# Scores as plain fp32 products of both heads in turn, block rows computed once and shifted by transfers, and another order in the mixer of a two-layer trunk

## The chip, the cores and the metric

The kernel runs on one core of a Trainium2 chip. The metric is the device time of one execution in microseconds (us), the median of several. Five engines work beside each other, each through its own instructions in order: TensorE (PE in the profile; its weight loads are PEld), VectorE (DVE), ScalarE (ACT), GpSimd (POOL) and SyncE (SP), which here only issues transfers (DMAs).

## The reference, cut to what matters

```python
# layer 0: h = x @ w_in + b; u, q, k, v = split(h)          x: 512 x 1024, each part 512 wide
# S5 on u: 32 groups of 16 channels, a complex state of 64 per group
lam_bar = exp(lam * dt); b_bar = (lam_bar - 1) / lam * b
states = scan(s[t] = lam_bar * s[t-1] + b_bar @ u[t])
y = gelu(real(c @ states) + d * u);  s5_out = val * sigmoid(gate) of y @ w_glu + b_glu
# stick-breaking attention, 8 heads of 64
z = q @ k.T * 64 ** -0.5                                    # strictly causal
log_keep = where(strict, log_sigmoid(-z), 0)
after = sum of log_keep over the keys between a key and its query
out = where(strict, exp(log_sigmoid(z) + after), 0) @ v
# x = LN(alpha * x + concat(s5_out, out) @ w_out + b), then a squared-ReLU MLP
# layer 1: conformer convolution (GLU, depthwise conv 31, LN, swish), then the MLP again
```

## The kernel before, in words

Channels lie on the 128 partitions and the 512 time steps along the free side. Products with weights are made in three parts: a weight chunk is fetched whole (`raw`), ACT rounds it to the fp32r format (`whi`), DVE takes the rest (`wlo`), inputs are split likewise (`xh`, `xl`), and PE adds `whi*xh`, `whi*xl`, `wlo*xh`. One result of 128 x 512 takes 8 x 3 = 24 such products. Weight chunks come in the order in which the program uses them, their fetches on SP's queue.

The mixer (layer 0 up to the MLP) is the first 254 us. Its parts are written down in the string `ORDER`. `sN` is stage N of the four S5 stages (`s5_states`, 4 tiles r of 128 channels' states each): DVE makes the block matrices `Gx` and `Cx` (time is cut in blocks of 4 steps); PE transposes `Gx` (`gp`) and forms the inner block matrix `tp`, which ACT copies to `Tx`; PE makes `vR`, `vI`; DVE turns them by cosine and sine tables, scans, turns them back and writes the shifted states `Sx` (the chain of tiles `m`, `n`). `yN` (`s5_outputs`) is then `yp = Tx*U + Cx*Sx` on PE, taken into `U` by DVE. `qN` (`qkv`) makes q, k, v of a pair of heads. `aN` (`attention`) is that pair's attention: scores `z` in groups A, B, C of key blocks for each head; `sp` = softplus of z (ACT: Abs, Exp, Ln; DVE: one addition; POOL: the causal mask), its parts `sh`, `sl`; `weigh` adds on PE the sums after each key; ACT takes Exp (`w`), POOL masks, and `values` makes the product with v (`av`). `gelu` works on all stages' `U` and turns the layout by way of DRAM (`Yd`, `yf`, parts `yh`, `yl`); `glu` is the S5 output projection (`gg`, `gv`); `acmo` are the products of the output projection. `ATT` gives the order of scores (s), weighing (w) and values (v) within one attention.

A scheduler places instructions of parts that stand near each other in the program on the engines, so that products of one part stand between those of another; the engines then run that order.

Of the kernel before, what the change touches and what calls it, by code (L numbers as in the profile page):

```python
# [16 lines left out]
P = 128  # L17
T = 512
# [29 lines left out]
ATT = "sC0 sA0 sB0 sB1 wC0 wB0 sC1 wB1 vB sA1 wA0 wC1 vC wA1 vA"  # L48
MIX_BUFS = (3, 4, 1, 4, 3)
WARM = 24  # L50
QK_BUFS = (1, 1)
TABLES_FIRST = (0, 1, 2, 3)
ORDER = "q0 s0 y0 s1 y1 a0 rows q1 s2 y2 a1 s3 y3 q2 gelu a2 q3 glu a3".split()
# [112 lines left out]
def kernel(ctx: ExitStack, tc: tile.TileContext, a: dict, out: bass.AP):  # L166
# [87 lines left out]
    def zz(name):  # L254
        return psum("z", name, MIX_BUFS[1])

# [22 lines left out]
    with tc.high_priority():  # L279
        for j in range(KT):  # L280
            tag, bufs = (("spt", MIX_BUFS[3]), ("wt", MIX_BUFS[4]), ("qh", 1))[(0, 1, 0, 1, 0, 1, 0, 2)[j]]
            xt = att.tile([P, 4, P], F32, tag=tag, name=f"xin{j}", bufs=bufs)
            nc.sync.dma_start(xt, a["x"][0][:, P * j : P * (j + 1)].rearrange("(b p) f -> p b f", p=P))
            xin.append(xt)
# [71 lines left out]
    def stt(o, x, s, y, op0, op1):  # L356
        V.scalar_tensor_tensor(o, x, s, y, op0=op0, op1=op1)  # L357
        return o
# [147 lines left out]
    def s5_states(q):  # L506
# [18 lines left out]
        for r in range(4):  # L525
            for t in range(4):
                for i in range(2):
                    PE.matmul(tp[32 * t : 32 * t + 32, r * P + 32 * t : (r + 1) * P],
                              Gx[:, i, r, 3].rearrange("p g q -> p (g q)"),
                              Cx[:, i, r, 0 : 4 - t].rearrange("p t g q -> p (t g q)"),  # L530
                              start=i == 0, stop=i == 1, tile_position=(0, 32 * t))
        tpv = tp.rearrange("p (r c) -> p r c", r=4)
        for t in range(4):
            pp = slice(32 * t, 32 * t + 32)
            S.copy(Tx[pp, :, 32 * t :], tpv[pp, :, 32 * t :])
# [92 lines left out]
    def qkv(p):  # L628
        r = []
        for s, n in enumerate("qkv"):  # L630
            ps, b = in_proj(4 + 4 * s + p, f"{n}{p}")
            if s == 2:
                t_ = att.tile([P, T], F32, tag=n, name=f"{n}{p}")
                act(t_, ps, AF.Identity, bias=b)
            else:
                b = b if s else bq8[:, p : p + 1]
                t_ = tuple(att.tile([P, T], F32R, tag=n + x, name=f"{n}{x}{p}", bufs=QK_BUFS[s]) for x in "hl")
                act(t_[0], ps, AF.Identity, bias=b)
                stt(t_[1], ps, b, t_[0].bitcast(F32), ALU.add, ALU.subtract)
            r.append(t_)  # L640
        return r
# [3 lines left out]
    def attention(p, q_, k_, v_):  # L645
# [21 lines left out]
        def scores(g):  # L667
            z = zs[g] = zz(f"z{p}{g}")
            for h, kb, o in groups[g]:
                R = slice(64 * h, 64 * h + 64)  # L670
                for i, (u, v) in enumerate(((0, 0), (0, 1), (1, 0))):
                    ins = PE.matmul(z[:, o : o + T - P * kb], k_[u][R, P * kb : P * kb + P], q_[v][R, P * kb :],
                                    start=o == 0 and i == 0, stop=i == 2, skip_group_check=True).ins
                    if o or i:
                        tc.add_manual_dep(ins, opened, NOSYNC, reason="the bank's first product")
                    opened = ins.name
            n = H if g[0] == "C" else T
            z = z[:, :n]
# [6 lines left out]
            hi = att.tile([P, n], F32R, tag=f"sh{g[0]}", name=f"sh{p}{g}", bufs=1)  # L685
            lo = att.tile([P, n], F32R, tag=f"sl{g[0]}", name=f"sl{p}{g}", bufs=1)
# [558 lines left out]
```

## Time and profile before

| | |
|---|---|
| median of 3 runs | 1217.15 us (1216.98 to 1217.62) |
| profiled execution | 1217.5 us, its span 1215.8 us |
| PE busy | 1187.4 us, 98% of the span |
| PEld, DVE, ACT, POOL busy | 83%, 65%, 46%, 5% |
| chain that ended last | PE 83%, DVE 10%, ACT 4%, DMA 2% |

The span lies within the execution; 1.7 us are around it. A matmul's duration in the trace is its time from issue to its modelled end, and the next starts before that; what one costs PE is the distance from its start to the next start. A plain fp32 matmul stands in the trace as two instructions, an fp32r one as one.

### The profile page before, as it was taken

The numbers are of one execution on the slowest core, as the hardware profiler recorded it, in microseconds if no ns is written. First come the engines' busy times: TensorE is split into PE (matmuls) and PEld (weight loads), VectorE is DVE, ScalarE is ACT, GpSimd is POOL, SyncE is SP. The second block draws the span as 40 slices with busy tenths as digits, with TensorE's granted clock in tenths as the row PEclk, the third lists the DMA queues.
The fourth block names the chain that finished last, engine by engine and source line by source line (L and its number), as shares of the span: only waits on it lengthen the run. The fifth ranks groups of instructions, "written<-read, shape, count | busy, mean of one in ns | idle before, by whom it ended". The sixth has DMA issues, their size and how long they took to land.

```text
span 1215.8 us, 16751 instructions
## 1 busy us (share of the span) xinstructions
PE 1187.4 (98%) x6546; PEld 1007.5 (83%) x6546; DVE 786.9 (65%) x1400; ACT 557.1 (46%) x990; POOL 58.2 (5%) x125
## 2 busy tenths in 40 slices
PE   9899999999999999999999999899999999999997
PEld 7677776789988888888999888889988888888885
DVE  7998774578745635646566999998843443434446
ACT  6836665734525524425323456964651332323230
POOL 1001101100000000000022110102000000000000
PEclk9999999999999999999999999999999999999999
DMA  8510042150878787887454631406142232323211
GB/s 205 155 49 22 19 130 61 31 195 1 264 250 282 251 284 264 270 283 268 165 183 159 213 104 36 139 1 208 39 152 87 87 108 83 122 70 121 70 52 69
DMA packets 128943, 168.86 MB, mean 139 GB/s; under 512 B 11298, under 2 KB 101666, under 8 KB 128864
## 3 DMA queue, kind: packets, MB, share of 16 engines
q1 hardware_dynamic: 120064, 136.30, 34.5%
q0 software_dynamic: 8640, 31.46, 7.6%
q8 instruction: 51, 0.84, 0.3%
q14 instruction: 28, 0.23, 0.1%
q10 hardware_dynamic: 160, 0.03, 0.0%
HBM read 132.12 MB, written 35.65 MB: 138 GB/s over the span
## 4 chain that ended last, share of the span: by engine, by line
PE 83%; DVE 10%; ACT 4%; DMA 2%; issue 1%; POOL 0%; SPq 0%; DVEq 0%; POOLq 0%; ACTq 0%
PE f L225 23%; PE g L1175 12%; PE acf L225 11%; PE fl L225 5%; PE tld L225 4%; PE tlb L225 4%; PE h L1159 3%; PE cv L1076 2%; PE pv L225 2%; PE pg L225 2%; PE tla L225 2%; PE pl L225 2%; DVE cz L357 1%; PE acmo L225 1%; PE av L709 1%
## 5 line engine op out<-in xcount | busy, mean ns | idle before, releaser
L102 DVE TENSOR_TENSOR wlo<-raw,whi 128x1024 fp32r<-128x1024 f32 x176 | 213.4, 1224 | 199.5 <-ACT whi L101 198.7
L101 ACT CAST whi<-raw 128x1024 fp32r<-128x1024 f32 x176 | 182.1, 1049 | 313.5 <-PE g L1175 107.4
L1175 PE MATMUL g<-whi,hh 128*128 128x512 f32 x208 | 81.8, 393 | 0.0
L1175 PE MATMUL g<-wlo,hh 128*128 128x512 f32 x208 | 81.8, 393 | 0.0
L1175 PE MATMUL g<-whi,hl 128*128 128x512 f32 x208 | 81.7, 393 | 0.0
L225 PE MATMUL f<-xah,whi 128*128 128x512 f32 x208 | 81.2, 390 | 0.0
L225 PE MATMUL f<-xdl,whi 128*128 128x512 f32 x208 | 81.1, 390 | 0.0
L225 PE MATMUL f<-xah,wlo 128*128 128x512 f32 x208 | 81.0, 390 | 0.0
L225 PE MATMUL f<-xdh,whi 128*128 128x512 f32 x208 | 81.0, 390 | 0.0
L225 PE MATMUL f<-xal,whi 128*128 128x512 f32 x208 | 81.0, 390 | 0.0
L225 PE MATMUL f<-xdh,wlo 128*128 128x512 f32 x208 | 81.0, 390 | 0.0
L225 PE MATMUL acf<-hl,whi 128*128 128x512 f32 x192 | 75.7, 394 | 0.0
L225 PE MATMUL acf<-hh,wlo 128*128 128x512 f32 x192 | 75.6, 394 | 0.0
L225 PE MATMUL acf<-hh,whi 128*128 128x512 f32 x192 | 75.5, 393 | 0.0
L215 ACT CAST hh<-fr 128x512 fp32r<-128x512 f32 x64 | 39.7, 621 | 59.6 <-DVE fr L353 59.6
L216 DVE TENSOR_TENSOR hl<-fr,hh 128x512 fp32r<-128x512 f32 x64 | 44.1, 690 | 31.9 <-ACT hh L215 31.8
L357 DVE SCALAR_TENSOR_TENSOR cy<-hp,wdw,cy 128x512 f32<-128x512 f32 (+1 forms) x99 | 63.6, 654 | 0.2
L357 DVE SCALAR_TENSOR_TENSOR cz<-hp,wdw,cz 128x512 f32<-128x512 f32 (+1 forms) x93 | 60.0, 656 | 0.0
L353 DVE TENSOR_TENSOR fr<-fr 128x512 f32<-128x512 f32 x64 | 43.7, 685 | 14.7 <-ACT fr L154 14.6
L1175 PEld LDWEIGHTS g<-wlo,hh 128*128 128x128 f32 x208 | 39.1, 188 | 8.9
L1175 PEld LDWEIGHTS g<-whi,hl 128*128 128x128 f32 x208 | 39.1, 188 | 8.9
L1175 PEld LDWEIGHTS g<-whi,hh 128*128 128x128 f32 x208 | 39.1, 188 | 8.8
(684 smaller groups left out, 3093.4 us busy)
## 6 DMA issues: line engine op xcount, KB each, us to landing
raw<-in_ffn_w_dram SPq DMA_DIRECT2D x48, 1024.0 KB, 5.8
raw<-in_ffn_w_dram SPq DMA_DIRECT2D x32, 512.0 KB, 3.5
kepth<-whi SPq DMA_DIRECT2D x30, 512.0 KB, 8.6
keptl<-wlo SPq DMA_DIRECT2D x30, 512.0 KB, 9.4
whi<-kepth POOLq DMA_DIRECT2D x30, 512.0 KB, 3.7
wlo<-keptl POOLq DMA_DIRECT2D x30, 512.0 KB, 4.5
raw<-in_conv_w_pw_dram SPq DMA_DIRECT2D x12, 1024.0 KB, 6.5
raw<-in_mix_w_in_dram SPq DMA_DIRECT2D x16, 512.0 KB, 3.9
```

Of the source, the lines that this page charges most:

```text
L101: i0 = nc.scalar.copy(hi, raw).ins
L102: i1 = nc.vector.tensor_sub(lo, raw, hi.bitcast(F32)).ins
L215: i0 = S.copy(hi, src).ins
L216: i1 = V.tensor_sub(lo, src, hi.bitcast(F32)).ins
L225: ins = PE.matmul(ps[:, c0:c1], u[:, k, ksl], v[:, c0:c1], start=start and k == 0 and i == 0, stop=stop and k == n - 1 and i == 2).ins
L353: V.tensor_tensor(o, x, y, op=op)
L357: V.scalar_tensor_tensor(o, x, s, y, op0=op0, op1=op1)
L709: ins = PE.matmul(av[R, P * kb :], vt[:, kb, R], ws_[f"{c}{h}"][0][:, o : o + T - P * kb], start=summed[h] == 1, stop=summed[h] == 4, skip ...
L1076: PE.matmul(cps[j][:, c0:c1], u, v[:, t + c0 : t + c1], start=t == 0 and i == 0, stop=t == n - 1 and i == 2)
L1159: PE.matmul(ps, u, v, start=k == 0 and i == 0, stop=k == nk - 1 and i == 2)
L1175: PE.matmul(pss[b], u, v[:, kk, :], start=k + kk == 0 and i == 0, stop=k + kk == nb - 1 and i == 2)
```

## The change

Four things. `qkv` makes plain fp32 q and k by one ACT instruction each, where before ACT made the rounded part (`qh`, `kh`) and DVE the rest (`ql`, `kl`). `scores` makes for each key block one fp32 product instead of three fp32r ones, head 0 (rows 0 to 63 of PE) and head 1 (rows 64 to 127) in turn; groups C and B of both heads stand ahead of A. In `s5_states`, `tp` is made once for the first block column: 8 matmuls on 4 column groups of PE instead of 32; ACT copies it to `tk`, and 16 DMAs on SP's queue place it in `Tx`, shifted. `ORDER` is another, and some buffer counts go with it.

```diff
-ATT = "sC0 sA0 sB0 sB1 wC0 wB0 sC1 wB1 vB sA1 wA0 wC1 vC wA1 vA"
-MIX_BUFS = (3, 4, 1, 4, 3)
+ATT = "sC sB wC0 wC1 vC wB1 wB0 sA wA0 vB wA1 vA"
+MIX_BUFS = (3, 4, 1, 3, 3)
+SP_BUFS = {"A": 1, "B": 2, "C": 2}
-ORDER = "q0 s0 y0 s1 y1 a0 rows q1 s2 y2 a1 s3 y3 q2 gelu a2 q3 glu a3".split()
+ORDER = "q0 s0 a0 y0 s1 q1 y1 a1 s2 y2 rows s3 y3 q2 q3 gelu a2 glu a3".split()
...
         tp = s5ps(f"tp{q}")
-        for r in range(4):
-            for t in range(4):
-                for i in range(2):
-                    PE.matmul(tp[32 * t : 32 * t + 32, r * P + 32 * t : (r + 1) * P],
-                              Gx[:, i, r, 3].rearrange("p g q -> p (g q)"),
-                              Cx[:, i, r, 0 : 4 - t].rearrange("p t g q -> p (t g q)"),
-                              start=i == 0, stop=i == 1, tile_position=(0, 32 * t))
-        tpv = tp.rearrange("p (r c) -> p r c", r=4)
+        for i in range(2):
+            for r in range(4):
+                PE.matmul(tp[32 * r : 32 * r + 32, :P], Gx[:, i, r, 3].rearrange("p g q -> p (g q)"),
+                          Cx[:, i, r, 0:4].rearrange("p t g q -> p (t g q)"),
+                          start=i == 0, stop=i == 1, tile_position=(0, 32 * r))
+        tk = s5.tile([P, P], F32, tag=("cii", "cix")[q % 2], name=f"tk{q}")
+        S.copy(tk, tp[:, :P])
         for t in range(4):
-            pp = slice(32 * t, 32 * t + 32)
-            S.copy(Tx[pp, :, 32 * t :], tpv[pp, :, 32 * t :])
+            for r in range(4):
+                nc.sync.dma_start(Tx[32 * t : 32 * t + 32, r, 32 * t :], tk[32 * r : 32 * r + 32, : P - 32 * t])
...
-            if s == 2:
-                t_ = att.tile([P, T], F32, tag=n, name=f"{n}{p}")
-                act(t_, ps, AF.Identity, bias=b)
-            else:
-                b = b if s else bq8[:, p : p + 1]
-                t_ = tuple(att.tile([P, T], F32R, tag=n + x, name=f"{n}{x}{p}", bufs=QK_BUFS[s]) for x in "hl")
-                act(t_[0], ps, AF.Identity, bias=b)
-                stt(t_[1], ps, b, t_[0].bitcast(F32), ALU.add, ALU.subtract)
+            t_ = att.tile([P, T], F32, tag=n, name=f"{n}{p}", bufs=2 if s == 2 else QK_BUFS[s])
+            act(t_, ps, AF.Identity, bias=b if s else bq8[:, p : p + 1])
...
-        def scores(g):
-            z = zs[g] = zz(f"z{p}{g}")
-            for h, kb, o in groups[g]:
-                R = slice(64 * h, 64 * h + 64)
-                for i, (u, v) in enumerate(((0, 0), (0, 1), (1, 0))):
-                    ins = PE.matmul(z[:, o : o + T - P * kb], k_[u][R, P * kb : P * kb + P], q_[v][R, P * kb :],
+        def scores(c):
+            for h in range(2):
+                zs[f"{c}{h}"] = zz(f"z{p}{c}{h}")
+            before = None
+            for pair in zip(groups[c + "0"], groups[c + "1"]):
+                for h, kb, o in pair:
+                    R = slice(64 * h, 64 * h + 64)
+                    ins = PE.matmul(zs[f"{c}{h}"][:, o : o + T - P * kb], k_[R, P * kb : P * kb + P], q_[R, P * kb :],
+                                    start=o == 0, stop=True, skip_group_check=True).ins
+                    if before:
+                        tc.add_manual_dep(ins, before, NOSYNC, reason="both heads in turn")
+                    before = ins.name
+            for h in range(2):
+                softened(f"{c}{h}")
...
-            hi = att.tile([P, n], F32R, tag=f"sh{g[0]}", name=f"sh{p}{g}", bufs=1)
-            lo = att.tile([P, n], F32R, tag=f"sl{g[0]}", name=f"sl{p}{g}", bufs=1)
+            hi = att.tile([P, n], F32R, tag=f"sh{g[0]}", name=f"sh{p}{g}", bufs=SP_BUFS[g[0]])
+            lo = att.tile([P, n], F32R, tag=f"sl{g[0]}", name=f"sl{p}{g}", bufs=SP_BUFS[g[0]])
```

`softened` is the rest of the old `scores`: softplus, mask and split, unchanged.

DVE, stage 0, where it makes `Cx` for the first `tp`. Before:

```order
L353 TENSOR_TENSOR Gx<-cm 64x16x16 x2
L353 TENSOR_TENSOR cm<-PW,Cd 128x320 x2
L353 TENSOR_TENSOR Cx<-cm 64x20x16
L102 TENSOR_TENSOR wlo_751<-raw_748,whi_750 128x1024
L357 SCALAR_TENSOR_TENSOR kl_745<-k_719,PB,kh_744 128x512
L353 TENSOR_TENSOR Cx<-cm 64x20x16
L353 TENSOR_TENSOR cm<-PW,Cd 128x320 x2
L357 SCALAR_TENSOR_TENSOR Cx<-cm 64x20x16 x2
L353 TENSOR_TENSOR cm<-EE,Braw 128x256 x2
L102 TENSOR_TENSOR wlo_1213<-raw_1210,whi_1212 128x1024
```

Now:

```order
L354 TENSOR_TENSOR Gx<-cm 64x16x16 x2
L354 TENSOR_TENSOR cm<-PW,Cd 128x320 x2
L354 TENSOR_TENSOR Cx<-cm 64x20x16 x2
L103 TENSOR_TENSOR wlo_747<-raw_744,whi_746 128x1024
L354 TENSOR_TENSOR cm<-PW,Cd 128x320 x2
L358 SCALAR_TENSOR_TENSOR Cx<-cm 64x20x16 x2
L354 TENSOR_TENSOR cm<-EE,Braw 128x256 x2
L103 TENSOR_TENSOR wlo_1136<-raw_1133,whi_1135 128x1024
```

The piece of k (`kl`, and just ahead of these rows that of q, `ql`) is gone, and the two first halves of `Cx` stand together, ahead of the weight rest `wlo`.

SP, the queue behind the last weight chunk (`raw`) of the second pair of heads. Before, fetches alone:

```order
L71 DMA raw_1280<-in_mix_w_in_dram 128x8x128
L71 DMA raw_1721<-in_mix_w_in_dram 128x8x128
L71 DMA raw_1756<-in_mix_w_in_dram 128x8x128
L621 DMA rows<-in_s_b_glu_dram 8x128
L621 DMA rows<-in_mix_b_out_dram 8x128
```

Now:

```order
L72 DMA raw_1199<-in_mix_w_in_dram 128x8x128
L537 DMA Tx<-tk_820 32x128 x4
L537 DMA Tx<-tk_820 32x96 x4
L537 DMA Tx<-tk_820 32x64 x4
L537 DMA Tx<-tk_820 32x32 x4
L72 DMA raw_1641<-in_mix_w_in_dram 128x8x128
L537 DMA Tx<-tk_1083 32x128 x4
L537 DMA Tx<-tk_1083 32x96
L72 DMA raw_1674<-in_mix_w_in_dram 128x8x128
L537 DMA Tx<-tk_1083 32x96 x3
```

All 16 shifts of stage 0 and those of stage 1 stand between weight fetches, which wait behind them in the queue.

PE, from the end of the last stage's `yp` to the first weighing of the third pair of heads (`z2C<-sh2B`). Before, the last rows ahead of it; between them and the last `yp` stand 50 more rows, 14 of them scores and all others products of q and k of the fourth pair:

```order
L225 MATMUL k_2103<-x0l_256,whi_1793 128x512
L225 MATMUL k_2103<-x0h_255,wlo_1794 128x512
L225 MATMUL k_2103<-x0h_268,whi_1793 128x512
L225 MATMUL k_2103<-x0l_269,whi_1793 128x512
L225 MATMUL k_2103<-x0h_268,wlo_1794 128x512
L225 MATMUL v_2138<-x0h_172,whi_2064 128x512
L696 MATMUL z2C_1901<-sh2B_1943,negs 128x128
L696 MATMUL z2B_1930<-sh2B_1943,negs 128x128
```

Now, all rows behind `yp`:

```order
L226 MATMUL v_1812<-x0h_268,wlo_1743 128x512
L644 MATMUL vt_1908<-ident,v_1738 128x128 x4
L671 MATMUL z2C_1916<-q_1672,k_1705 128x256
L671 MATMUL z2C_1917<-q_1672,k_1705 128x256
L671 MATMUL z2B_1941<-q_1672,k_1705 128x384
L671 MATMUL z2B_1942<-q_1672,k_1705 128x384
L671 MATMUL z2B_1941<-q_1672,k_1705 128x128
L671 MATMUL z2B_1942<-q_1672,k_1705 128x128
L226 MATMUL gg_2073<-yh_1856,whi_1808 128x512
L226 MATMUL gg_2073<-yl_1857,whi_1808 128x512
L226 MATMUL gg_2073<-yh_1856,wlo_1809 128x512
L699 MATMUL z2C_1916<-sh2B_1953,negs 128x128
```

The 42 products of the fourth pair's q, k, v that stood ahead of the weighing are made earlier, beside stages 2 and 3; in their place stand one product of v, three of the S5 output projection (`gg`, which need `yh` and `yl`) and the scores.

## Rows read from the trace of the kernel before

**Rows 1.** The page: busy time of each engine with its share of the span, and the chain of work that ended last.

```profile
PE 1187.4 (98%) x6546; PEld 1007.5 (83%) x6546; DVE 786.9 (65%) x1400; ACT 557.1 (46%) x990; POOL 58.2 (5%) x125
PE 83%; DVE 10%; ACT 4%; DMA 2%; issue 1%; POOL 0%; SPq 0%; DVEq 0%; POOLq 0%; ACTq 0%
```

**Rows 2.** Busy time of the engines in stretches of the mixer: stretch and length, then us busy and (x instructions) of each engine, PE's granted clock as a share of full speed, DMA share, GB/s.

```profile
60.00:80.00 20.00, 19.31 (x165) 16.41 (x168) 19.62 (x37) 3.90 (x7) 0.70 (x1) 1.00 0.19 53
80.00:100.00 20.00, 18.76 (x118) 15.01 (x111) 19.16 (x35) 14.48 (x28) 2.69 (x7) 1.00 0.21 59
...
0.00:254.00 254.00, 241.24 (x1428) 187.51 (x1428) 189.71 (x410) 158.23 (x285) 26.28 (x65) 0.99 0.33 89
```

**Rows 3.** PE in order of time in stage 1 (start, us, instructions, and in brackets the idle time before with what ended it), and the group of all `tp` in the mixer (busy us, mean ns, idle).

```profile
77.94 0.83 PE L542 MATMUL vI<-U,gt 128*128 128x128 f32 x6
78.71 1.72 PE L528 MATMUL tp<-Cx,Gx 128*32 128x128 f32 x62
80.35 0.49 PE L542 MATMUL vI<-U,gt 128*128 128x128 f32 x2
...
L528 PE MATMUL tp<-Cx,Gx 128*32 128x128 f32 (+3 forms) x256 | 9.3, 259 | 2.7 <-DVE Cx L357 1.5 <-DVE Cx L353 1.3
```

**Rows 4.** PE in order of time in the last `yp`: the distance from start to start gives what a 128 x 128 fp32 instruction costs.

```profile
160.64 0.61 PE L572 MATMUL yp<-Sx,Cx 128*128 128x128 f32 x4
161.09 0.39 PE L570 MATMUL yp<-U,Tx 128*128 128x128 f32 x2
```

**Rows 5.** PE and then DVE in order of time in stage 0, and the windows view of the stretch at the lower clock.

```profile
55.09 0.38 PE L528 MATMUL tp<-Cx,Gx 128*32 128x128 f32 x2 [1.27 <-DVE Cx L353]
56.94 2.95 PE L528 MATMUL tp<-Cx,Gx 128*32 128x128 f32 x62 [1.48 <-DVE Cx L357]
...
48.81 0.75 DVE L357 SCALAR_TENSOR_TENSOR ql<-q,bq,qh 128x512 fp32r<-128x512 f32 x1
53.70 0.73 DVE L357 SCALAR_TENSOR_TENSOR kl<-k,PB,kh 128x512 fp32r<-128x512 f32 x1
55.90 0.98 DVE L357 SCALAR_TENSOR_TENSOR Cx<-cm 64x320 f32<-64x320 f32 x2
...
56.09:59.51 3.42, 2.57 (x60) 2.45 (x62) 2.68 (x5) 0.06 (x1) 0.00 (x0) 0.50 0.29 87
```

**Rows 6.** PE's busy time with score products alone, all 96 of them, then PE in order of time where the two heads of group B meet (the fourth pair), and the pair of `av` products on column halves.

```profile
sum 254.00, PE 19.14; mean PE 4.79
...
218.23 0.33 PE L672 MATMUL z3B<-qh,kl 64*128 64x384 f32 x1
218.23 0.44 PE L672 MATMUL z3B<-qh,kh 64*128 64x384 f32 x2
...
110.08 1.53 PE L709 MATMUL av<-w0A,vt 128*64 128x512 f32 x4
111.54 0.66 PE L520 MATMUL gp<-ident,Gx 128*128 128x128 f32 x4
```

**Rows 7.** DVE in order of time: the first and the last of the chain from `vR` to `Sx` in stage 0; SP's queue (issue times); and from the list of transfers KB of each and median us from issue to landing.

```profile
61.24 0.68 DVE L353 TENSOR_TENSOR m<-vR,tc 128x512 f32<-128x512 f32 x1
71.21 0.69 DVE L353 TENSOR_TENSOR Sx<-m,n 128x508 f32<-128x508 f32 x1
...
49.42 1.74 SPq L607 DMA_DIRECT2D U<-Ud  x4
...
U<-Ud SPq DMA_DIRECT2D x16, 64.0 KB, 4.4
rows<-in_ffn_b_dram SPq DMA_DIRECT2D x2, 8.0 KB, 1.8
```

**Rows 8.** From the end of the last `yp` to the first weighing of the third pair: PE, DVE, ACT and POOL in order of time, then the windows view of that stretch for the products with weights (x42) and for the scores (x14).

```profile
162.52 0.38 PE L672 MATMUL z2C<-qh,kl 64*128 64x256 f32 x1
174.73 0.27 PE L696 MATMUL z2C<-sh2B,negs 128*128 128x128 f32 x1
...
170.20 1.23 DVE L102 TENSOR_TENSOR wlo<-raw,whi 128x1024 fp32r<-128x1024 f32 x1 [1.97 <-ACT whi L101]
172.69 0.68 DVE L357 SCALAR_TENSOR_TENSOR sp2B<-z2B,sp2B 128x512 f32<-128x512 f32 x1
...
167.52 1.28 ACT L156 ACT_TABLE_LOAD   x1
174.00 0.62 ACT L215 CAST sh2B<-sp2B 128x512 fp32r<-128x512 f32 x1
...
173.44 0.53 POOL L664 TENSOR_SCALAR_AFFINE_SELECT sp2B<-sp2B 128x256 f32<-128x256 f32 x1 [0.31 <-DVE sp2B L357]
...
162.52:174.73 12.21, 9.93 (x42) 1.00 0.46 115
162.52:174.73 12.21, 2.49 (x14) 1.00 0.46 115
```

**Rows 9.** PE's waits in the first 255 us: engine, line, what it waited for, us in total, times, longest.

```profile
PE yp L572 <- DVE Sx L353: 1.9, 3, 0.7
PE z2C L672 <- ACT w2C L160: 1.2, 1, 1.2
```

**Rows 10.** The one other stretch at the lower clock, and the one ahead of it.

```profile
779.00:783.10 4.10, 0.29 (x1) 0.19 (x1) 4.10 (x12) 3.10 (x7) 1.00 (x2) 1.00 1.08 372
783.10:786.50 3.40, 3.29 (x14) 3.03 (x14) 3.21 (x10) 2.62 (x9) 0.00 (x0) 0.50 0.04 14
```

More of the change, by code (lines that the diff above doesn't have):

```diff
@@ L280 @@
         for j in range(KT):
-            tag, bufs = (("spt", MIX_BUFS[3]), ("wt", MIX_BUFS[4]), ("qh", 1))[(0, 1, 0, 1, 0, 1, 0, 2)[j]]
+            tag, bufs = (("spt", MIX_BUFS[3]), ("wt", MIX_BUFS[4]), ("q", 1), ("k", 1))[(0, 1, 0, 1, 0, 1, 3, 2)[j]]
             xt = att.tile([P, 4, P], F32, tag=tag, name=f"xin{j}", bufs=bufs)
@@ L665, in mask, with softened @@
                                    base=0, channel_multiplier=-1).ins.name
-        def scores(g):
-            z = zs[g] = zz(f"z{p}{g}")
-            for h, kb, o in groups[g]:
-                R = slice(64 * h, 64 * h + 64)
-                for i, (u, v) in enumerate(((0, 0), (0, 1), (1, 0))):
-                    ins = PE.matmul(z[:, o : o + T - P * kb], k_[u][R, P * kb : P * kb + P], q_[v][R, P * kb :],
[L673 to L676, printed above, removed]
+        def scores(c):
[12 more added lines that the diff above has]
+                softened(f"{c}{h}")
+        def softened(g):
             n = H if g[0] == "C" else T
-            z = z[:, :n]
+            z = zs[g][:, :n]
             sp = att.tile([P, T], F32, tag="spt", name=f"sp{p}{g}", bufs=MIX_BUFS[3])[:, :n]
```

## The prediction

> **What bounds the kernel now.** I read the page first: PE is busy for 98% of the span and carries 83% of the chain that ended last [rows 1]. So a change is worth what it takes from PE's work, or from PE's waits. The windows view then says where PE waits at all: of the first 254 us, which hold the whole mixer and everything that changes, PE works 241.2 [rows 2]; the rest of the kernel keeps its instructions. In the same windows DVE works 19.6 and 19.2 of 20 us between 60 and 100 us. There DVE is nearly as full as PE, and work taken from it can start PE sooner. Last I read PE's waits by what ended them: for `Sx` 1.9 us, for `w2C` 1.2, and little for any other [rows 9]. PE is filled so well because each chain of DVE and ACT lies beside products of q, k and v that need nothing from it. The change moves just these products, so besides the work removed the question is which chain stays without cover.
>
> All sums are made against the profiled execution's own 1217.5 us; the median of the runs shown, 1217.15, lies 0.35 below it, and I take that off at the end.
>
> **Inner block matrix.** All 256 instructions of `tp` keep PE busy for 9.3 us [rows 3]. In stage 1, 62 of them take 78.71 to 80.35, 1.64 us. One 128 x 128 fp32 instruction costs about 0.11 us from start to start (4 begin at 160.64, the next at 161.09) [rows 4]. The widths of `tp` are 128, 96, 64 and 32, so 62 in a row would take 62 x 80/128 x 0.11 = 4.3 us. It goes 2.6 times faster: the four column groups run at once. The group with the widest products alone (16 of 128 columns, 1.8 us) would take what all take, so the time looks like that of the longest group. After the change each stage has 16 instructions of 128 columns, four on each column group: 0.45 us if the groups go on running together, 1.8 if they do not. By the row nearest to it I take 0.55, four stages 2.2. At full clock `tp` now costs about 7.5 (the 9.3 hold some 1.8 of stage 0, which is slow for another reason, below). **Gain 5.3**, bounds 0.3 and 5.7.
>
> The copies to `Tx` leave ACT, and 16 DMAs each stage take their place. Four small DMAs take SP 1.74 us to issue, 0.43 each, so 16 take 6.9; such transfers land 1.8 (8 KB) to 4.4 us (64 KB) after issue [rows 7]; the new ones have 16 KB at most, and I take 2. `Tx` is wanted by `yp`, which also waits for `Sx`: that chain takes DVE 61.24 to 71.9, over 10 us, in stage 0 [rows 7]. 6.9 + 2 = 8.9 is hidden behind it by about 1 us, so I cost it at nothing. If the cover is gone (a weight fetch between two shifts, which waits for its buffer and holds SP's queue), what is late next is `yp`, then `U` on DVE; that is a rival below.
>
> **Start of stage 0.** PE stands for 1.27 and 1.48 us ahead of `tp`, both times for `Cx` [rows 5]. On DVE the rests of q and k, 0.75 and 0.73 us, stand ahead of the last `Cx`; both go, so `Cx` comes 1.5 us sooner: **gain 1.5** (bounds 0.7, if ACT is late next, and 2.75, the whole wait). [...] I expect the wait that is left, some 1.3 us with 16 instructions behind it, not to bring it: **gain 1.3** (bounds 0 and 1.3). The other six rests of q and k give DVE 4.5 us more room in stretches where it is full; PE's 1.9 us for `Sx` are what this can reach, and I count 1.
>
> **Scores.** The 96 score instructions, 24 for a pair of heads, keep PE busy for 19.1 us [rows 6]; since each runs past the start of the next, by starts it is about 18, or 4.5 a pair. After the change a pair has 8 matmuls, 16 instructions, 1280 columns a head. At the pitch of [rows 4] 128 columns cost 0.22 as an fp32 matmul: 10 x 0.22 = 2.2 us a head. If the heads run one behind the other that is 4.4, almost what it is now; if they overlap fully, 2.2. Two places speak for overlap: where the heads meet in group B, instructions of both start at the same 218.23; and the two `av` products, on halves of PE's columns and plain fp32, take 110.08 to 111.54, 1.46 us, where four instructions of 512 columns would take 4 x 0.44 = 1.76 [rows 6]. That fits an order in which the second half of head 0's product and the first of head 1's run together: three units for a lone pair, two for each more in a row. Groups C and B stand together so (about 1.6 us), A's two products stand apart in three of four pairs (1.7). That is 3.3, and some 0.2 for places where another product comes between: four pairs 14, **gain 4.0** (bounds 0.3 and 9).
>
> Scores take half of PE's rows and `tp` a quarter of its columns, so PE changes between these and whole-array products. In [rows 3] six instructions of `vI` take 77.94 to 78.71, 0.77 instead of 0.66: about 0.1 us for such a change. [...] With some 20 more changes at 0.1 the sum would be 2 us worse; by the row alone, where as many changes go as come, nothing.
>
> **Order.** The costly part. From the end of the last `yp` to the first weighing of the third pair of heads, 162.52 to 174.73, 12.2 us pass now: `U`, the last block of gelu, ACT's table load for Exp at 167.52, softplus, `sh2B` at 174.00 [rows 8]. PE is busy throughout, with 42 products of q, k, v (9.9 us) and 14 of scores (2.5) [rows 8]. After the change one product of v, the transposes of v, six score matmuls and three `gg` stand there, and these last wait for `yl`, which comes after softplus too. The chain itself becomes about 1.5 longer, since a weight rest (1.23 us [rows 8]) stands between the first and the other `U` on DVE and ACT has both heads' group C ahead of B. So 13.7 us against some 5.2 of PE work (0.2 + 0.5 + 3 + 0.7, and 0.8 for a bank that frees late): **loss 8.5** (bounds 6 and 11). After a wait like this the clock falls as well: after 779.00 to 783.10, in which PE worked 0.29 us, it ran 3.40 us at 0.50 [rows 10]. That loses up to 1.7; part of it lies ahead of head 1's wait, and I count **0.9**.
>
> The products taken from there stand beside `a0` and stages 1 to 3. They are needed in any case, so they gain only what they fill: in `a0` the softplus of all groups stands behind stage 0's `Sx` on DVE. `Sx` ends near 68 (71.9 less 2.7 by the start of stage 0, less 1.2 for a weight rest that no longer stands in it); with additions 1.5, mask 0.5 and `sh2B`'s like 0.6 [rows 8] the first weighing can start near 71. PE, some 58.4 behind `vI`, has scores (2) and 35 products of 0.23 until then, to about 68.5: a wait of 2.5 to 3. Some 2 us more are new in `a1`. Against them go 1.9 and 1.2 [rows 9] and some 1.5 of smaller waits. I count nothing.
>
> **Sum.** -5.3 - 1.5 - 1.3 - 1.0 - 4.0 + 8.5 + 0.9 = -3.7 us: 1213.8 for the profiled execution, **1213.5** as a median.
>
> **Rivals.** *The order loses more than the work gives (slower).* If in `a0` and `a1` PE waits 5 us more than I count, and the wait behind the last `yp` is 11, the losses are 17.3 against gains of 13.1: +4, 1221. It decides from the point where PE's waits of these phases exceed what goes by 13. For it speaks that DVE is full between 60 and 100 us [rows 2], where `a0` now stands; against it, that DVE has 6 us less to do. *Shifts late (no change).* If fetches hold the queue so that `Tx` comes 1 to 1.5 us after `Sx` in three stages, 4 us go: 1217.5. [...] *Heads do not overlap (no change).* Then scores gain 0.3 instead of 4: 1217.2. *Heads overlap fully (more).* 2.2 a pair saves 9: 1208.5.
>
> **How the numbers follow.** The measurement can tell 0.2%, 2.4 us, from no change. Forecast 0.40 (of which 0.34 faster, 0.06 within), full overlap 0.10, shifts late 0.12, no overlap 0.08, order loses more 0.30. So faster 0.44, same 0.26, slower 0.30. The range reaches from full overlap with a smaller wait behind `yp` (1208.5 less 3, 1205.5) to the order's loss with the clock's whole loss on top (1221 and 2, 1223); the forecast's own is 1210 to 1216.5.
>
> **What would show it.** `tp` at or below 0.6 us a stage; in stage 0 one wait for `Cx` and no stretch at 0.50; scores at 3 to 3.6 us a pair, starts of both heads within 0.02 us; `yp` waiting for `Sx`, never for a DMA; one PE wait of 7 to 10 us behind the last `yp`, ended by `sh2B` or `yl`, with a slow stretch behind it. I am wrong if that wait is much shorter because the scheduler's filler or the chain differs from what I counted, or if PE waits over 5 us in `a0` or `a1`.

## The result and the profile after

The change made the kernel slightly slower: 1219.3 us in the median of 13 runs (1218.35 to 1224.55) beside 1217.13 for the kernel before on the same chip, a ratio of 1.0021 (95% interval 1.0012 to 1.0029), or 1.5 to 3.5 us. The forecast was 1213.5.

The profiled execution took 1218.93 us, its span is 1217.2. From the page and the windows view of the changed kernel (columns as in [rows 1, 2]):

```profile
PE 1183.1 (97%) x6322; PEld 998.9 (82%) x6322; DVE 779.9 (64%) x1392; ACT 552.3 (45%) x978; POOL 60.7 (5%) x125
...
0.00:254.00 254.00, 235.45 (x1198) 178.14 (x1199) 182.56 (x402) 152.99 (x273) 28.89 (x65) 0.97 0.33 90
```

In the first 254 us PE is busy 5.8 us less than in [rows 2], DVE 7.2 and ACT 5.2 less, and yet the mixer is longer. Its end is best read at the first product behind it: it starts at 255.07 us before and at 256.44 now, 1.4 later. From there to the end it is 960.7 and 960.8 us, so all of the difference lies in the mixer.

The busy time hides how much work went, since a product at a granted clock of 0.50 counts longer: in after a 128x512 fp32r product takes 0.43 us from start to start at 0.50 (72.50 to 72.93) and 0.23 at 1.00 (40.05 to 40.28). Counted from start to start, without idle time and with time at the lower clock by half, PE's work in the mixer fell from 240.2 to 231.0 us. That is 9.2 less; the forecast had 9.3. What came in its place is 5.8 us of waiting and 4.8 us lost to the clock. By stretches (this table is worked out from the starts and ends of PE's instructions in both traces, in us):

| term | forecast | measured |
|---|---|---|
| work: `tp` | -5.3 | -4.6 (7.7 to 3.1) |
| work: scores | -4.0 | -1.3 (17.9 to 16.6) |
| work: `av` -2.0, weighing -0.7, rest -0.6 | 0 | -3.3 |
| waits and clock up to the end of the last `yp` | -3.8 | +0.6 (10.0 to 10.5) |
| waits and clock from there to the first weighing of pair 2 | +8.5 | +8.1 (0 to 8.1) |
| waits and clock behind it | +0.9 | +1.9 (3.4 to 5.3) |
| sum | -3.7 | +1.4 |

**The stretch behind the last `yp`.** PE in order of time in the changed kernel, then the windows view (the long wait, what follows at the lower clock, and behind it):

```profile
168.25 0.61 PE L574 MATMUL yp<-Sx,Cx 128*128 128x128 f32 x4
168.62 0.48 PE L226 MATMUL v<-x0h,wlo 128*128 128x512 f32 x1
168.94 0.60 PE L644 MATMUL vt<-ident,v 128*128 128x128 f32 x4
169.46 0.70 PE L671 MATMUL z2C<-q,k 64*128 64x256 f32 x4
170.87 1.51 PE L671 MATMUL z2B<-q,k 64*128 64x384 f32 x8 [0.70 <-ACT vt L646]
178.85 0.80 PE L226 MATMUL gg<-yh,whi 128*128 128x512 f32 x1 [6.47 <-ACT yh L155]
...
180.67 0.37 PE L699 MATMUL z2C<-sh2B,negs 128*128 128x128 f32 x1
...
168.70:180.67 11.97, 4.79 (x22) 2.74 (x21) 8.72 (x23) 10.15 (x21) 1.32 (x3) 0.72 0.62 168
178.85:187.50 8.65, 8.61 (x29) 7.24 (x30) 4.57 (x8) 4.84 (x10) 2.43 (x4) 0.50 0.39 121
187.50:191.00 3.50, 3.50 (x13) 1.36 (x12) 0.00 (x0) 1.81 (x4) 0.49 (x2) 0.99 0.00 0
```

This is the place that the prediction spoke of: one product of v, the transposes, the scores, and then one wait of 6.47 us. The stretch takes 11.97 us now and took 12.2 before [rows 8], although PE's busy time in it fell from the whole of it to 4.79. So it is not PE that sets its length. ACT is busy for 10.15 of it, and ACT and DVE do one thing after another:

```profile
170.33 0.86 DVE L358 SCALAR_TENSOR_TENSOR U<-U,par,yp 128x128 f32<-128x128 f32 x3
174.18 0.69 DVE L358 SCALAR_TENSOR_TENSOR g<-g,U 128x512 f32<-128x512 f32 x1 [0.39 <-ACT g L161]
...
174.17 1.28 ACT L157 ACT_TABLE_LOAD   x1
178.18 0.61 ACT L155 ACTIVATE yh<-yf 128x512 fp32r<-128x512 f32 x1
179.90 0.62 ACT L216 CAST sh2B<-sp2B 128x512 fp32r<-128x512 f32 x1 [0.32 <-POOL sp2B L660]
```

`U`, the last block of gelu, the table load for Exp and softplus are the chain of before; on ACT `yh` for `gg` comes only behind most of softplus.

**Ahead of it.** PE's waits up to the end of the last `yp`, changed kernel (columns as in [rows 9]), and a row of the kernel before:

```profile
PE z0C L699 <- ACT sh0B L216: 2.2, 1, 2.2
PE tp L530 <- DVE Cx L358: 1.5, 1, 1.5
PE yp L572 <- DMA raw<-in_mix_w_in_dram: 1.3, 1, 1.3
PE z0C L671 <- DVE m L354: 0.6, 1, 0.6
PE v L226 <- ACT ue L155: 0.5, 1, 0.5
PE yp L572 <- DMA Tx<-tk: 0.4, 1, 0.4
PE av L712 <- POOL w1C L660: 0.4, 1, 0.4
PE yp L572 <- ACT g L155: 0.4, 1, 0.4
PE yp L574 <- DVE Sx L354: 0.2, 1, 0.2
...
47.17 0.51 PE L225 MATMUL v<-x0h,whi 128*128 128x512 f32 x1 [1.75 <-ACT ue L154]
```

The waits for `Sx` (1.9 us in [rows 9], now 0.2) and for `Cx` (2.75 in [rows 5], now 1.5) shrank as forecast. In their place stand the first weighing's wait for `sh0B`, 2.2 us, and waits of `yp` for the shifted copies.

One of these waits most likely says nothing of the change. `v` waits for `ue` (ACT's copy of a part of `u`, near 47 us) 1.75 us in the profiled execution of before and 0.48 in that of after, but 0.98 to 1.85 in the eight other kernels whose `ORDER` begins like that of after. So the profiled execution of after starts this `v` 1.0 us earlier than before does, and from there to the mixer's end the change costs 2.4 us, not 1.4; the medians differ by 2.2.

### The profile page after: what moved, and what is told of

Its sections match the earlier page's. It is cut to its first block, busy times and chain, and to the rows that moved or that the text cites. A ratio compares the mean times of both kernels' runs of the same rounds, so it can differ in the third digit from the quotient of the medians.

```text
span 1217.2 us, 16366 instructions
## 1 busy us (share of the span) xinstructions
PE 1183.1 (97%) x6322; PEld 998.9 (82%) x6322; DVE 779.9 (64%) x1392; ACT 552.3 (45%) x978; POOL 60.7 (5%) x125
## 4 chain that ended last, share of the span: by engine, by line
PE 83%; DVE 8%; ACT 3%; issue 3%; DMA 2%; POOL 1%; DVEq 0%; SPq 0%; POOLq 0%; ACTq 0%
PE f L226 23%; PE g L1178 12%; PE acf L226 11%; PE fl L226 5%; PE tld L226 4%; PE tlb L226 4%; PE h L1162 3%; PE cv L1079 2%; PE pv L226 2%; PE pg L226 2%; PE tla L226 2%; PE pl L226 2%; DVE cz L358 1%; DMA raw<-in_mix_w_in_dram 1%; PE acmo L226 1%
## 5 line engine op out<-in xcount | busy, mean ns | idle before, releaser
L226 PE MATMUL acf<-hh,wlo 128*128 128x512 f32 x192 | 75.6, 394 | 0.0
```

The costliest lines, as they stand in the source:

```text
L226: ins = PE.matmul(ps[:, c0:c1], u[:, k, ksl], v[:, c0:c1], start=start and k == 0 and i == 0, stop=stop and k == n - 1 and i == 2).ins
```

## The experiments

All times are medians; each ratio is taken beside the kernel before as it ran with that kernel, so kernels are best compared by their ratios. The columns work, wait and clock are PE's in the mixer of the profiled execution, counted as above; mixer end is the start of the first product behind it.

| kernel | us | beside before: ratio (95%) | work | wait | clock | mixer end |
|---|---|---|---|---|---|---|
| before | 1217.1 | | 240.2 | 12.1 | 1.3 | 255.1 |
| after | 1219.3 | 1.0021 (1.0012 to 1.0029) | 231.0 | 17.8 | 6.0 | 256.4 |
| q3_behind | 1221.3 | 1.0033 (1.0020 to 1.0047) | 231.6 | 19.6 | 5.0 | 257.8 |
| dead_fill | 1221.2 | 1.0035 (1.0017 to 1.0053) | 229.9 + 5.9 dead | 13.7 | 6.7 | 257.9 |
| dead_until_weigh | 1223.2 | 1.0047 (1.0035 to 1.0060) | 232.0 + 8.3 dead | 15.3 | 0.0 | 257.2 |
| gelu_behind_a2 | 1233.1 | 1.0130 (1.0112 to 1.0148) | 232.1 | 28.4 | 8.2 | 270.3 |
| old_order | 1227.9 | 1.0079 (1.0063 to 1.0094) | 230.3 | 23.3 | 9.2 | 264.4 |
| tp_only | 1231.5 | 1.0118 (1.0098 to 1.0138) | 233.0 | 23.3 | 16.3 | 274.1 |
| scores_only | 1225.5 | 1.0061 (1.0044 to 1.0078) | 237.4 | 14.9 | 8.0 | 261.9 |
| heads_apart | 1220.1 | 1.0025 (1.0012 to 1.0037) | 231.7 | 18.6 | 5.9 | 257.7 |
| shifts_by_block | 1219.9 | 1.0024 (1.0013 to 1.0036) | 231.2 | 18.2 | 12.6 | 263.5 |
| attention_beside | 1227.1 | 1.0075 (1.0049 to 1.0102) | 231.1 | 22.6 | 6.3 | 261.5 |
| q1_early | 1228.3 | 1.0107 (1.0087 to 1.0127) | 232.8 | 20.4 | 7.6 | 262.4 |
| gelu_and_shifts | 1238.1 | 1.0172 (1.0147 to 1.0197) | 232.0 | 26.6 | 11.4 | 271.6 |

Executions of one kernel differ by some us: the profiled one of shifts_by_block took 1227.1, 7 us above its median, those of tp_only (1236.8) and dead_fill (1225.4) 5 and 4 above theirs, and that of dead_until_weigh 1219.5, the shortest of its six. Their mean granted clock goes along: 0.984 in the profiled execution of shifts_by_block and 0.988 to 0.991 in its others, 0.984 and 0.987 in those of tp_only and dead_fill, the lowest of either kernel, and 0.996 in that of dead_until_weigh, 0.990 to 0.993 in its others. So columns of one row are compared with care, and sums are not made across rows.

### Is it the wait behind the last `yp`?

The theory after the result was that the order had opened this wait, and that filling it would bring the forecast gain back. **q3_behind** puts the products of q, k and v of the last pair behind the weighing of the third, as before.

```diff
-ORDER = "... s3 y3 q2 q3 gelu a2 glu a3"
+ORDER = "... s3 y3 q2 gelu a2 q3 glu a3"
```

> The changed kernel with one word of ORDER moved: q3 stands behind gelu and a2 again. If the loss comes from the uncovered wait behind the last yp and the low clock after it, the 6.5 us wait and the 13.7 us at half clock (4.3 us of work lost) go, less what opens where q3's products stood (2 to 5 us): 1208 to 1212. If the order is not the cause and the new parts are simply worth less than counted: 1217 to 1220.

It took 1221.3 us. PE in order of time in that kernel:

```profile
171.80 1.13 PE L671 MATMUL z2B<-q,k 64*128 64x384 f32 x6
179.48 0.79 PE L226 MATMUL gg<-yh,whi 128*128 128x512 f32 x1 [6.55 <-ACT yh L155]
```

The scheduler drew the products forward all the same: of the pair's 72 products 6 stand between the last `yp` and the first weighing, where before had 42, and the hole is still 6.55 us. So this run does not test the theory. The order names phases; which product fills which wait is dealt out by the scheduler.

**dead_fill** keeps every instruction of the changed kernel in its place and fills the hole with 52 products that nothing reads.

```diff
+            if p == 2 and c == "B":
+                for i in range(52):
+                    ins = PE.transpose(av[:, :P], ident, ident).ins
+                    tc.add_manual_dep(ins, before, NOSYNC, reason="dead products in turn")
+                    before = ins.name
+                dead.append(before)
...
+                        if dead:
+                            tc.add_manual_dep(ins, dead.pop(), NOSYNC, reason="behind the dead products")
```

> The changed kernel with 52 dead transposes of the identity (0.11 us each, 5.7 us) on PE in the long wait behind the last scores of the third pair; every other instruction stands where it stood on each engine. [...] If the chain of ACT and DVE behind the wait sets the end whatever PE's clock is: within 1 us of 1219.3. If the dead work itself delays the first weighing: later by 0.5 or more.

PE in order of time, and the windows view, of dead_fill:

```profile
173.53 5.90 PE L681 MATMUL av<-ident 128*128 128x128 f32 x52
180.08 0.50 PE L226 MATMUL gg<-yh,whi 128*128 128x512 f32 x1 [0.65 <-ACT yh L155]
...
181.80 0.33 PE L706 MATMUL z2C<-sh2B,negs 128*128 128x128 f32 x1 [0.18 <-ACT sh2B L216]
...
182.36:189.19 6.83, 6.66 (x26) 6.40 (x26) 2.70 (x5) 2.91 (x6) 1.69 (x3) 0.50 0.34 88
```

The first weighing comes as late as without the 5.9 us of extra work (11.99 us from the start of the last `yp` instruction, 12.08 in after), which shows that PE had nothing to say there. The lower clock, 0.50, did not go; it came later, behind waits of 0.65, 0.30, 0.18 and 0.29 us, and lasted 6.83 us. From the first weighing to the mixer's end it is 76.05 us, 75.77 in after: no gain.

**dead_until_weigh** fills longer, with 74 products, so that PE works until the first weighing is ready; three products of `gg` then stand behind it.

```diff
-                for i in range(52):
+                for i in range(74):
```

> As the run with 52 dead transposes, but 74 of them (8.3 us), so that PE has work up to the first weighing and the first gg stand behind it. With 52 the low clock only moved from 173.9 to 182.4, behind the short waits that were left (0.65, 0.3, 0.2, 0.3 us), and as much work lay in it. If idle time of PE is what brings the low clock, none is left here: no stretch at 0.5 between 170 and 195, and 3.3 us less than the changed kernel, near 1216. If the low clock comes after such a place whatever PE does: a stretch of 6.8 us or more and 1219 to 1221 again.

Here the profiled execution has no stretch at 0.50 in the whole mixer (the windows row below, clock 1.00):

```profile
173.26 8.30 PE L681 MATMUL av<-ident 128*128 128x128 f32 x74
181.53 0.33 PE L706 MATMUL z2C<-sh2B,negs 128*128 128x128 f32 x1
...
184.97 0.33 PE L706 MATMUL z2C<-sh2B,negs 128*128 128x128 f32 x1 [1.23 <-ACT sh2B L216]
...
0.00:254.00 254.00, 238.01 (x1269) 181.40 (x1270) 182.76 (x401) 152.92 (x273) 29.35 (x65) 1.00 0.33 90
```

And still the mixer ends at 257.15, where after has 256.44. 1.2 us of that is the later start of `v` (47.32 against 46.13); from there it is 0.5 us shorter than after. From the first weighing it takes 75.6 us, 0.2 less than in after, with 0.7 us more of `gg` in it: so the lower clock behind the hole, where 8.6 us of products ran at 0.50, cost under 1 us. The last row says why: at full speed PE stands 1.23 us for head 1's `sh2B`. The softplus chain sets the pace there, through ACT, DVE and POOL in turn (in after ACT itself stands 1.10 us for POOL's mask ahead of that `sh2B`), and a slow PE merely fills the waits. So of the 4.3 us which the account above books as lost to the clock there, little comes back at full speed. Behind the first weighing PE waits 3.6 us here and 1.8 in after; and part of the 4.3 is bookkeeping, since at 0.50 products took less than twice as long (eight of head 1's weighing, start to start, 1.92 us in after and 1.15 here).

The clock at `a0` is another matter. In after and dead_until_weigh the same instructions stand there, and both wait 2.2 us for `sh0B`; from the first weighing to the last instruction of the first stage's `yp` it is 16.2 us in after, with this stretch,

```profile
71.48:74.90 3.42, 3.42 (x13) 3.04 (x13) 3.10 (x7) 1.85 (x4) 0.21 (x1) 0.50 0.44 133
```

and 14.8 without it. There PE is full, and the clock costs 1.4 us.

**gelu_behind_a2** shortens the chain itself: with the weighing of the third pair ahead of gelu, its softplus need not wait for gelu's last block and the table load.

```diff
-ORDER = "... q2 q3 gelu a2 glu a3"
+ORDER = "... q2 q3 a2 gelu glu a3"
```

> The changed kernel with gelu behind a2 in ORDER. On ACT and DVE the third pair's softplus then stands ahead of the last block of gelu and its table load, so the chain from the last yp to the first weighing gets shorter by about 5 us (12 to 7), and the S5 output products are no longer wanted ahead of it. If that chain is what opened the wait of 7.2 us: the wait is 2 to 3 us, and 1214 to 1217, if what is late next (gelu, and gg behind a2) takes only part of it back. If it takes it all back: 1218 to 1221.

PE's waits in that kernel:

```profile
PE gg L226 <- ACT yh L155: 8.7, 2, 7.3
PE z2C L699 <- ACT sh2B L216: 4.9, 1, 4.9
```

The weighing waits only 4.9 us, but `gg`, which needs gelu, then waits 8.7. The same chain is late for another reader: 1233.1 us. These two are 13.6 us beside the 6.5 of after, 7 of the 10.6 by which all waits grew.

### The parts one by one

**tp_only** is the kernel before with the new `tp`, `tk` and shifts alone; **scores_only** is the changed kernel with the old `tp` and the old order; **old_order** is the changed kernel with the old order alone.

```diff
# old_order, and scores_only with it
-ORDER = "q0 s0 a0 y0 s1 q1 y1 a1 s2 y2 rows s3 y3 q2 q3 gelu a2 glu a3"
+ORDER = "q0 s0 y0 s1 y1 a0 rows q1 s2 y2 a1 s3 y3 q2 gelu a2 q3 glu a3"
# scores_only besides (and tp_only the other way, from the kernel before)
-        tk = s5.tile([P, P], F32, tag=("cii", "cix")[q % 2], name=f"tk{q}")
-        S.copy(tk, tp[:, :P])
...
+            S.copy(Tx[pp, :, 32 * t :], tpv[pp, :, 32 * t :])
```

> The kernel before with the new tp, tk and the 16 transfers a stage alone. By the traces tp falls from 8.8 to 2.8 us from start to start, of which 1.3 is the low clock of stage 0: 1211 to 1213. If the transfers come late for yp in each stage (1 to 1.5 us each): 1214 to 1217.

> The kernel before with the new scores, ATT and buffers alone, old tp and old ORDER. Scores from 18 to 16.4 us and 1.4 less of the wait for Cx: 1213 to 1215. If the two heads overlapped as I had predicted (14 us): 1211 to 1213. If heads do not overlap: 1216 to 1217.5.

> The changed kernel with the whole ORDER of before; tp, shifts, scores and ATT stay new. Order as the cause: the parts keep their gains (tp 5.9, Cx 1.4, scores 1.5), 1207 to 1211. Parts worth nothing: 1216 to 1219.

All three are slower than both kernels, by 7 to 14 us beside the kernel before, though each has less PE work than it. In tp_only and old_order PE waits 23.3 us instead of 12.1; in scores_only 14.9. The clock takes 16.3, 9.2 and 8.0 us by the account, 1.3 before. The waits are of the same kind but in other places. Two rows of old_order:

```profile
PE q L226 <- ACT v L155: 4.2, 2, 2.7
PE z0C L699 <- ACT sh0B L216: 4.1, 1, 4.1
```

What follows: given the new parts, the new order is worth some 7 us (ratios 1.0079 against 1.0021), where the prediction booked it as a loss of 9.4. And no part could be valued by itself here: each edit lets the scheduler deal the filling products anew (in tp_only PE's rows differ from the middle of stage 0 on). Why tp_only waits in just those places was not traced further. Part of these times lies outside the mixer: in scores_only, old_order and dead_fill there are two stretches of 6.8 us at 0.50 between 786 and 811 us, where after has one of 3.4 (784.9 to 788.3).

### The heads

**heads_apart** makes all of head 0's products of a group and then head 1's.

```diff
-            for pair in zip(groups[c + "0"], groups[c + "1"]):
+            for pair in (groups[c + "0"], groups[c + "1"]):
```

> The changed kernel with each group's products of head 0 first and then those of head 1, not in turn. If the turn makes the heads overlap (three units of time for a pair instead of four), B's three stretches get longer by about 0.3 us a pair, C and A stay (one product a head), so 0.5 to 1.5 us slower than 1219.3. If nothing overlaps: the same as 1219.3 within 0.5.

PE's work for scores rose only from 16.6 to 17.1 us. The edit changes less than I meant: groups A and C have one product a head, so only B's order differs, and it is B of the first two pairs that got longer (1.76 to 2.02 and 1.90 to 2.12). In the fourth pair B took 1.07 us here too, and by their starts products of both heads still ran side by side, 13 ns apart. The question is answered by rows of after itself. PE in order of time where head 0's A stands alone, where both heads' A stand together (second pair), and where B's eight instructions stand together (fourth pair), each with the next row:

```profile
75.38 1.12 PE L671 MATMUL z0A<-q,k 64*128 64x512 f32 x2
76.43 0.49 PE L226 MATMUL k<-x0h,whi 128*128 128x512 f32 x1
...
124.19 1.13 PE L671 MATMUL z1A<-q,k 64*128 64x512 f32 x4
125.48 0.87 PE L712 MATMUL av<-w1B,vt 128*64 128x384 f32 x4 [0.16 <-POOL w1B L660]
...
217.99 1.14 PE L671 MATMUL z3B<-q,k 64*128 64x384 f32 x8
219.06 0.50 PE L226 MATMUL acmo<-gh,whi 128*128 128x512 f32 x1
```

One head's A takes 1.05 us alone; both together take 1.13. So the heads do overlap, almost fully, in the A pair and in the fourth pair's B. Eight B instructions take 1.07 together (fourth pair), but 1.76 and 1.90 in the first two, where something stands between, and 1.51 in the third, where they stand together right behind a wait (170.87 in the rows further up). What makes it longer there is not shown. Full overlap would be 0.70 + 1.07 + 1.13 = 2.9 us a pair, 11.6 in all; 16.6 were measured, because A stands apart in three of four pairs (2.10 instead of 1.13 each) and B takes longer in three.

### The shifts

SP's queue in the changed kernel in order of time, stages 0 and 1, and from the list of transfers (stretch 50 to 170 us) the largest and the smallest shift:

```profile
56.96 10.08 SPq L537 DMA_DIRECT2D Tx<-tk  x16
...
94.57 3.55 SPq L537 DMA_DIRECT2D Tx<-tk  x5
98.21 0.53 SPq L72 DMA_DIRECT2D raw<-in_mix_w_in_dram  x1
98.80 5.64 SPq L537 DMA_DIRECT2D Tx<-tk  x9
104.54 0.53 SPq L72 DMA_DIRECT2D raw<-in_mix_w_in_dram  x1
105.11 1.22 SPq L537 DMA_DIRECT2D Tx<-tk  x2
...
Tx<-tk SPq DMA_DIRECT2D x16, 16.0 KB, 2.1
Tx<-tk SPq DMA_DIRECT2D x16, 4.0 KB, 1.7
```

Sixteen shifts take SP 10.08 us, 0.63 each, not the 0.43 that I took from [rows 7]. In stage 1 two weight fetches (512 KB each) stand between them. The semaphore events of the trace show what the second of these does, issued at 104.54 and landed at 108.82: the last two shifts, issued behind it from 105.11 and 105.75, land at 109.00 and 109.18, over 3.4 us after issue, and `yp` goes on at 109.09 behind a wait of 1.3 us. The profile puts that wait down to `raw`, but PE's weight load just ahead waited until 109.04 for the semaphore of a shift. **shifts_by_block** issues the shifts by block, so that the first blocks of `yp` have theirs first.

```diff
-        for t in range(4):
-            for r in range(4):
+        for r in range(4):
+            for t in range(4):
```

> The changed kernel with the 16 shifts of a stage issued block by block (all four of r = 0 first), so that the first products of yp find their part of Tx after four shifts, not after thirteen. If the late shifts cost what PE's waits for Tx and the fetch between them show (2.4 us in three stages): 1 to 2 us less, 1217.3 to 1218.3. If PE then waits for Sx instead: 1219.3 within 0.5.

PE's waits in that kernel:

```profile
PE gg L226 <- ACT yh L155: 3.7, 1, 3.7
...
PE yp L574 <- DVE Sx L354: 1.1, 2, 0.5
...
PE yp L572 <- DMA Tx<-tk: 0.7, 1, 0.7
```

`yp`'s waits for DMAs fell from 1.7 to 0.7 us, and `Sx` is late next: 1.1 instead of 0.2. The median, 1219.9 (ratio 1.0024 beside 1.0021), cannot be told from that of after. So the late shifts were a real wait with almost nothing to win behind it. The shorter `gg` wait is of this execution, which has a stretch of 17.07 us at 0.50 ahead of it (74.27 to 91.34), where after has 3.42.

### Other orders

```diff
# attention_beside
+ORDER = "q0 s0 y0 s1 a0 y1 q1 s2 a1 y2 rows q2 s3 a2 y3 gelu q3 glu a3"
# q1_early
+ORDER = "q0 s0 a0 q1 y0 s1 y1 a1 s2 y2 rows s3 y3 q2 q3 gelu a2 glu a3"
# gelu_and_shifts: the orders of gelu_behind_a2 and shifts_by_block at once
```

> The changed kernel with another ORDER: each attention stands beside the next S5 stage (q0 s0 y0 s1 a0 y1 q1 s2 a1 y2 rows q2 s3 a2 y3 gelu q3 glu a3). Behind the last yp 30 products of the fourth pair (6.8 us) and its scores stand ahead of gg. If the uncovered wait and the clock behind it are the loss, 6.5 + 4.3 us go, less 3 to 5 for waits elsewhere: 1211 to 1214. If every order leaves the same sum of waits because DVE's and ACT's chains set the pace: 1217 to 1221.

> The changed kernel with q1 ahead of y0 in ORDER (q0 s0 a0 q1 y0 s1 y1 a1 ...). The wait for the first weighing stays as it is (35 products stand ahead of it as before), later places change. If the sum of PE's waits is set by DVE's and ACT's chains: 1218 to 1221. If this order only were bad: 1215 or less.

> Both edits of the two runs beside it. If the two waits are independent, both gains: 1212 to 1216. If one chain of DVE and ACT sets the pace through all of it, no more than the better of the two.

They took 1227.1, 1228.3 and 1238.1 us, all slower than after. No version here beats either kernel. These three, and tp_only, scores_only, old_order and gelu_behind_a2 as well, lie above every range that was named for them: how the scheduler deals the filling products was not foreseen in any of them, and it is not explained here.

## Why the prediction was wrong

**The step that failed** is the paragraph on the order, where the new waits of `a0` and `a1` were set against waits that go, with "I count nothing", together with the shifts, costed at nothing. Up to the end of the last `yp` the forecast had waits and clock fall by 3.8 us; they rose by 0.6. This miss of 4.4 is most of the 5.1 by which the sum was off. The gains booked at the start of stage 0 are not in it: they came (`Cx` 1.3 of 1.5, the clock 1.3 of 1.3). The 1.3 for the clock is half of the 2.57 us that PE works at 0.50 in [rows 5]; no run shows that half by itself, and what the runs showed is that stretch of 3.42 us in before and none in stage 0 of after. The miss is made of three things:

- The same wait twice. New waits of 3.7 us came in `a0` and `a1`, less than the 4.5 to 5 counted. But of the 4.6 set against them only 1.8 was left: the 1.9 us for `Sx` gave 1.0 as a gain of its own, and stood again in the offset; the 1.2 for `w2C` lies behind the hole, not ahead of it; and the smaller waits gave 1.2 of 1.5. That is a rise of 1.9 where nothing was counted.
- The clock. A new stretch at 0.50 came at 71.48, behind the wait for `sh0B` that I had forecast, and no clock was counted for it: 1.7 us of PE, 1.4 of them on the path by the comparison with dead_until_weigh.
- The shifts, costed at nothing with a cover of "about 1 us". `yp` waits 1.3 + 0.4 us for DMAs. The term was 16 x 0.43 + 2 = 8.9; the trace gives 16 x 0.63 + 2 = 12, and over 3.4 instead of 2 for shifts behind a weight fetch. One shift takes 0.63 us to issue and lands 1.7 to 2.1 us after issue, so that in a row of 16 the issuing, 10.08 us, is the larger part. This was the rival "shifts late", and it has the right mechanism at under half of its price (1.7 of 4 us); shifts_by_block shows that behind it `Sx` is late anyway.

These add up to 5.3 us. Another 0.7 of waits stands ahead of `yp` for other things and 0.2 of `Cx` did not come, and 1.7 went the other way by the execution, above all in `v`'s wait for `ue`: the 0.6 is that much flattered.

**What was right.** The wait behind the last `yp` was forecast at 8.5 by counting the chain of `U`, gelu, table load and softplus, less PE's work beside it; waits and clock there came to 8.1, 6.47 of it in one wait, ended by `yh`, with a slow stretch from within it on. The mechanism is right, the closeness in part luck: the chain took 12.1 us, not 13.7, and PE's work beside it was 4.0, not 5.2. `a0`'s wait was forecast at 2.5 to 3, and 2.2 + 0.6 came. In stage 0 one wait for `Cx` was left (1.47, forecast some 1.3) and no stretch at 0.50. PE's total work fell by 9.2 where 9.3 was forecast, but that is luck, as the terms show.

**Mis-sized terms.** `tp` takes 3.1 us, not 2.2, within its bounds; PE needs 0.78 a stage. Scores gained 1.3, not 4.0. The overlap that this term doubted is there; what I mis-sized is the lone product (1.05 us, I had taken 0.85) and how often B is split (2.6 for C and B in the first two pairs, 2.2 in the third; I had 1.6). The two heads' products, on different halves of PE's rows, ran beside each other in the A pair: 1.13 us against 1.05 for one. The miss was made good by a gain that I had not seen: in three of four pairs the eight `av` products of group B run in one piece on both column halves now, 1.01 us where they took 1.67 to 1.87; in the fourth they are still split (1.80). All `av` products in the mixer took 16.61 us of PE in the kernel before and take

```profile
sum 257.00, PE 14.65; mean PE 14.65
```

now. Behind the first weighing I counted 0.9 for the clock; waits and clock rose by 1.9 there. Most of it stands for the pace of softplus and not for the clock, as dead_until_weigh shows.

**The rivals.** "Order loses more" (1221) came nearest in time, but not by its mechanism: `a0` and `a1` wait 2.8 and 0.9 us, no more than was counted, and the hole is 8.1, not 11. (Its losses add up to 11 + 0.9 + 5 = 16.9, not 17.3; its time stays 1221.) "Heads do not overlap" fell by the A pair. "Full overlap" has the right mechanism but is reached only in places.

**What lies under it.** The reading "a change is worth what it takes from PE's work, or from PE's waits" took the two as separate. Before, PE was busy for 241 of 254 us because 288 products of q, k and v lay beside chains of DVE and ACT that are nearly as long. With 9.2 us less PE work the chains are as long as they were, and what was work becomes waiting. That is shown at one place by the 11.97 against 12.2 us with less than half of the work in it, and by dead_fill, where 5.9 us of extra PE work cost nothing there. For the mixer as a whole it is argued from the table, one execution each: thirteen kernels with 230 to 238 us of real work, and none ends before the one that has 240, not even dead_until_weigh, which lost nothing to the clock. What each late chain costs by itself, and why the old order suits the new parts so badly, stays open.

## What to carry to other kernels

An engine that is busy 98% of the time may be filled rather than limiting: before booking a cut of its work as a gain, count at each chain beside it how much filler would be left, since work that is taken away shows up as waiting where the chain is as long (here 5.8 us more of waiting for 9.2 less of work). Put each wait that goes into the sum once, and give every new wait of a few us its own line for the clock behind it (here 13.7 us at 0.50 came with the wait of 6.47, and 0 to 17.1 with that of 2.2), on the path only if PE, and not a chain beside it, sets the pace there. Where a scheduler deals the filler, single parts of a change cannot be added up: run the whole.

## What the runs showed of the hardware

- The stretch at a granted clock of 0.50 with the 6.47 us wait lasted 13.7 us in after (173.9 to 187.5, from 1.5 us into the wait on), where [rows 10] had 3.40 after 4.10 us in which PE worked 0.29. The wait of 2.2 us for `sh0B` was followed by 3.42 us at 0.50 in after, by 6.83 in dead_fill, by 17.1 in shifts_by_block and by none in dead_until_weigh; the wait of 1.47 in stage 0 of after by none.
- In after, beside dead_until_weigh, a stretch at 0.50 with 8.6 us of products in it cost under 1 us where the softplus chain set the pace, and one with 3.4 us cost 1.4 where PE was full.
- A transfer of 4 to 16 KB from `tk` to `Tx` took SP 0.63 us to issue in after, one of 64 KB (`U<-Ud`) 0.43 in before [rows 7]: the smaller ones took longer.
- In stage 1 of after two shifts of 4 KB issued right behind a 512 KB fetch on the same queue landed 3.4 and 3.9 us after issue, just behind the fetch; the median of the 4 KB shifts is 1.7.
- In after an fp32 product on half of PE's rows with 512 columns took 1.05 us alone (75.38 to 76.43), and both halves' together 1.13, to the modelled end of the last: the other half's added at most 0.08.
